# One-hot rows of the PEER gate matrix move from GpSimd to VectorE and ScalarE; row gathers run five ahead

## The chip, the cores and the metric

The kernel runs on one core of one Trainium2 chip. The metric is device time in microseconds (us), the median of several executions. A core has five engines with an instruction queue each: TensorE (PE in the profile; PEld is its weight load), VectorE (DVE), ScalarE (ACT), GpSimd (POOL), and the DMA queue's own engine SyncE (SP). Each engine works through its queue strictly in order and waits on semaphores for what other engines or transfers must deliver.

## The reference

Two transformer blocks over 512 tokens of width 1024 (the second one two layers deep). The change touches one part of the first block, a PEER feed-forward with 16384 experts of one row each. Cut to that part:

```python
q  = (hn @ w_query).reshape(b, s, 8, 2, 128)
sc = einsum('bshcd,hckd->bshck', q, sub_keys)        # 8 heads, 2 x 128 keys
v1, i1 = top_k(sc[..., 0, :], 16);  v2, i2 = top_k(sc[..., 1, :], 16)
cand = v1[..., :, None] + v2[..., None, :]           # 256 pairs, 16 best kept
top, pos = top_k(cand.reshape(..., 256), 16)
idx  = i1 * 128 + i2 at pos;  gate = softmax(top)    # 8 x 16 experts per token
act  = gelu(einsum('bld,blhkd->blhk', hn, expert_down[idx]))
out  = einsum('blhk,blhkd->bld', gate * act, expert_up[idx])
```

So every token picks 128 of 16384 experts, takes a dot product with each one's down row, and sums their up rows with weight gate times gelu.

## The kernel before

The first 128 tokens (`GAT`) are done by **gathering**: for each of the 128 slots one indirect DMA fetches 128 down rows (512 KB, one per token), VectorE multiplies and reduces them against `hn` (line 1049), and after 128 such steps 128 more fetch the up rows, which VectorE adds into `racc` (line 1058). GpSimd issues these gathers (line 1045), with a ring of four `rows` buffers, so a gather may only be issued when the row four steps earlier has been consumed.

The other 384 tokens (`DENSE`) are done **densely**: all 16384 experts are computed. `peer_down` runs 128 dense rows; a dense row streams 512 KB of down weights through SyncE's queue, splits them into a high part on ScalarE (`whi`, line 267) and a low part on VectorE (`wlo`, line 268), runs 24 matmuls of 128x384 (lines 272 to 274), applies Gelu on ScalarE (line 1124) and writes 192 KB of `actd` to DRAM from ScalarE's DMA queue (line 1125). Then `peer_up` runs 16 groups of 8 tiles, each tile again 24 matmuls, with the `actd` values multiplied by a gate matrix read back from DRAM (`gd`, line 1162).

That **gate matrix** is 128 x 128 per token, and `peer_gates` builds it during the dense rows of `peer_down`: per token a one-hot matrix `oa` (line 1280) and a one-hot matrix scaled by the gates, `ob` (line 1282), each 128x128, are multiplied on TensorE (line 1283, two matmul instructions per token in the trace). Four tokens form a quad; a quad fills one PSUM bank that ScalarE copies out (`gst`, line 1284). 96 quads are needed, 384 tokens. After each 32 tokens GpSimd issues a 2 MB write to `gd` (line 1286). Of the four `oa` of a quad GpSimd makes three and VectorE one; all four `ob` are VectorE's.

The order on the queues: `hidden()` yields four pieces per dense row; after each piece the gate and routing work gets `PACE` credits (a quad costs 2.2, a routing step its yielded cost), and the gather generator `rows` gets 0.27 of a step. A tile scheduler then places the instructions on each engine by its own estimate of when they are ready, and may move gathers forward. In `peer_up` each tile is followed by 1.25 gather steps.

At the hand-over, the `at` and `gt` loads of the first `peer_up` group go through GpSimd's queue, behind the gathers that stand before them there, and TensorE's first `peer_up` matmul needs them.

Of the kernel before, what the change touches and what calls it, by code (L numbers as in the profile page):

```python
# [10 lines left out]
F32 = mybir.dt.float32  # L11
# [3 lines left out]
AF = mybir.ActivationFunctionType  # L15
ALU = mybir.AluOpType
# [6 lines left out]
D = 1024  # L23
# [12 lines left out]
FAR = CAP * (NEXP + 2)  # L36
FULL = (6, 11)
RAW = 20
PACE = 0.62
GAT = 128  # L40
DENSE = S - GAT

# [177 lines left out]
class Kernel:  # L220
# [813 lines left out]
    def gathered(self, st):  # L1034


        V, A, P, p = self.V, self.A, self.P, st["pool"]
        act = p.tile([128, 128], F32, name="ract")
        steps = [(name, k) for name in ("rows_down", "rows_up") for k in range(128)]
        ahead = []  # L1040
        for i, (name, k) in enumerate(steps):
            while len(ahead) < 4 and i + len(ahead) < len(steps):
                n, kk = steps[i + len(ahead)]
                r = p.tile([128, D], F32, name="rows", bufs=4)
                P.indirect_dma_start(r, None, self.I[n], bass.IndirectOffsetOnAxis(ap=st["idx"][:, kk:kk + 1], axis=0))  # L1045
                ahead.append(r)
            r = ahead.pop(0)
            if name == "rows_down":
                V.tensor_tensor_reduce(out=r, in0=r, in1=st["hn"], scale=1.0, scalar=0.0, op0=ALU.mult, op1=ALU.add,
                                       accum_out=act[:, k:k + 1])  # L1050
            else:
                if k == 0:
                    A.activation(act, act, AF.Gelu)
                    V.tensor_mul(act, act, st["gate"])
                    acc = p.tile([128, D], F32, name="racc", tag="rhn")
                    V.tensor_scalar(acc, r, act[:, 0:1], None, op0=ALU.mult)
                else:
                    V.scalar_tensor_tensor(acc, r, act[:, k:k + 1], acc, op0=ALU.mult, op1=ALU.add)  # L1058
            yield
        for h in range(2):  # L1060
            tr = self.ps("t", [128, 4, 128])
            for k in range(4):
                self.transpose(tr[:, k], acc[:, (4 * h + k) * 128:(4 * h + k + 1) * 128])
            x = self.x[:, 4 * h:4 * h + 4, :GAT]
            V.tensor_add(x, x, tr)

    def peer_down(self, actd, gd, TG, st, rows):

        V, A, P, T, Q, I = self.V, self.A, self.P, self.T, self.Q, self.I
        with self.pool("u2") as up:  # L1070
# [12 lines left out]
            with self.pool("pk", 1) as p1:  # L1083
# [23 lines left out]
                with self.pool("pk2", 2) as p2:  # L1107
# [18 lines left out]
                    for i, _ in enumerate(hidden()):  # L1126
                        credit += PACE
                        while credit > 0:
                            credit -= next(work, 1.0e9)
                        if st["ready"]:  # L1130
                            due += 0.27
                            while due >= 1:
                                next(rows, None)
                                due -= 1
                    _run(work)

    def peer_up(self, actd, gd, TG, rows):
        V, A, P, T, Q, I = self.V, self.A, self.P, self.T, self.Q, self.I
        with self.pool("pu", 2) as p2:
# [28 lines left out]
            for g in range(16):  # L1168
                hi, lo = _run(nxt)
                nxt = weighted(g + 1) if g < 15 else iter(())  # L1170
                for j in range(KC):
# [4 lines left out]
                        self.mm3(ps, (whi[:, sl], wlo[:, sl]), (hi[:, k], lo[:, k]), k == 0, k == 7)  # L1176
                    next(nxt, None)
                    V.tensor_add(self.x[:, j, GAT:], self.x[:, j, GAT:], ps)
                    due += 1.25
                    while due >= 1:  # L1180
                        next(rows, None)
                        due -= 1
# [86 lines left out]
    def peer_gates(self, c, sT, p2, gd, TG):  # L1269
# [3 lines left out]
        for j in range(128 // TG):  # L1273
            st = p2.tile([128, 128, TG], F32, name="gst")
            for t4 in range(TG // 4):
                ps = self.ps("ts"[t4 % 2], [128, 4, 128])
                for i in range(4):
                    t = j * TG + t4 * 4 + i
                    oa = p2.tile([128, 128], F32, name="oa", bufs=10)
                    (V if i == 3 else P).tensor_scalar(oa, iota, sT[:, 1, t:t + 1], None, op0=ALU.is_equal)  # L1280
                    ob = p2.tile([128, 128], F32, name="ob", bufs=10)
                    V.tensor_scalar(ob, iota, sT[:, 0, t:t + 1], sT[:, 2, t:t + 1], op0=ALU.is_equal, op1=ALU.mult)
                    T.matmul(ps[:, i], lhsT=oa, rhs=ob, start=True, stop=True)
                A.activation(st[:, :, t4 * 4:t4 * 4 + 4], ps.rearrange("p t i -> p i t"), AF.Copy)
# [827 lines left out]
```

## Time and profile before

| | us |
|---|---|
| median of 3 executions (lowest to highest) | 4601.32 (4599.44 to 4601.47) |
| the profiled execution's own time | 4597.02 |
| its span, first to last instruction | 4595.2 |
| TensorE busy in the span | 4302.3 (94%) |
| VectorE busy | 2733.3 (59%) |
| ScalarE busy | 1342.6 (29%) |
| GpSimd busy | 1489.9 (32%) |

The busy shares are means over stages of different kinds. The dense rows of `peer_down` run from about 945 us to 1673 us of the span, the gate matrix is built from 1088 us to 1556 us, and `peer_up` runs from 1704 us to about 2245 us. A window of the trace gives the busy time of each engine in one stretch, the granted TensorE clock (1.00 is 2.4 GHz, 0.50 is 1.2 GHz), and how busy the DMA engines were. Matmuls overlap, so the mean duration of one is longer than its share of the busy time.

### The profile page before, as it was taken

To read this page: it belongs to the slowest core of one execution; us is meant where nothing else is said; L and a number is where in the kernel's file an instruction comes from. 1 tells how busy PE (TensorE), PEld (TensorE's weight loads), DVE (VectorE), ACT (ScalarE), POOL (GpSimd) and SP (SyncE) were. 2 spreads that over 40 slices of the span, in tenths; PEclk is the share of its full clock that TensorE was granted. 3 is DMA by queue.
4 is the path that set the end of the run, shared out by engine and by line. 5 is a ranking of instruction groups with operands and counts; after the bars stand their busy time and mean duration, and the time that the engine had idled before them with its cause. 6 is when DMAs were issued, how large, how long until landed. Compare 5 with 4: busy or idle time off the path is not lost. (4 is left out here: it accounts for less than half of the span.)

```text
span 4595.2 us, 59880 instructions
## 1 busy us (share of the span) xinstructions
PE 4302.3 (94%) x21607; PEld 3280.4 (71%) x21607; DVE 2733.3 (59%) x5252; ACT 1342.6 (29%) x2195; POOL 1489.9 (32%) x1171
## 2 busy tenths in 40 slices
PE   8998989998899879999999998999989999899997
PEld 7787778897889869999877675444448778545443
DVE  6577775798877679997457775221234665522122
ACT  5324442343333323333333332000123433200001
POOL 2153345019999654342113451000011346100000
PEclk9999999999999989999999998999999999899998
DMA  4133433347778899996333446989862122598985
GB/s 155 50 103 109 128 113 112 108 141 253 274 275 300 316 350 350 340 334 237 118 116 114 138 133 223 364 321 346 319 256 85 61 67 95 218 353 325 350 311 236
DMA packets 351615, 987.39 MB, mean 215 GB/s; under 512 B 34288, under 2 KB 114672, under 8 KB 349392
## 3 DMA queue, kind: packets, MB, share of 16 engines
q1 hardware_dynamic: 293488, 795.77, 48.6%
q0 software_dynamic: 39392, 162.55, 9.9%
q10 hardware_dynamic: 18432, 25.17, 1.5%
q8 instruction: 174, 2.85, 0.3%
q14 instruction: 129, 1.06, 0.1%
HBM read 926.70 MB, written 56.66 MB: 214 GB/s over the span
## 5 line engine op out<-in xcount | busy, mean ns | idle before, releaser
L267 ACT ACTIVATE whi<-raw 128x1024 fp32r<-128x1024 f32 (+3 forms) x582 | 569.0, 979 | 1307.0 <-PE acc L273 780.2
L268 DVE TENSOR_TENSOR wlo<-raw,whi 128x1024 fp32r<-128x1024 f32 (+4 forms) x438 | 535.6, 1225 | 231.7 <-ACT whi L267 224.9
L1746 PE MATMUL acc<-raw,xg 128*64 128x512 f32 (+1 forms) x2024 | 554.7, 599 | 0.0
L349 POOL TENSOR_TENSOR ssq<-ssq,sq 128x512 f32<-128x512 f32 (+1 forms) x22 | 31.5, 1442 | 1337.1 <-ACT sq L348 1336.8
L272 PE MATMUL acc<-hn_hi,whi 128*128 128x384 f32 (+1 forms) x1152 | 406.5, 354 | 9.0 <-ACT act L1124 9.0
L274 PE MATMUL acc<-hn_hi,wlo 128*128 128x384 f32 (+1 forms) x1152 | 402.1, 350 | 13.5 <-DVE wlo L268 13.5
L268 POOL TENSOR_TENSOR wlo<-raw,whi 128x1024 fp32r<-128x1024 f32 (+3 forms) x144 | 281.1, 1954 | 373.9 <-ACT whi L267 363.7
L273 PE MATMUL acc<-hn_lo,whi 128*128 128x384 f32 (+1 forms) x1152 | 402.1, 349 | 0.0
L272 PE MATMUL acc<-c_hi,whi 128*128 128x384 f32 x1024 | 342.7, 336 | 30.2 <-ACT c_hi L267 30.2
L1746 PEld LDWEIGHTS acc<-raw,xg 128*64 128x64 f32 (+1 forms) x2024 | 164.0, 140 | 284.2 <-issue 260.8
L273 PE MATMUL acc<-c_lo,whi 128*128 128x384 f32 x1024 | 343.4, 335 | 0.6 <-DVE c_lo L268 0.6
L274 PE MATMUL acc<-c_hi,wlo 128*128 128x384 f32 x1024 | 342.4, 335 | 0.8 <-DVE wlo L268 0.8
L1280 POOL TENSOR_SCALAR oa<-const,sT 128x128 f32<-128x128 f32 x288 | 269.1, 946 | 2.8
L1794 DVE SCALAR_TENSOR_TENSOR x<-t,mod,x 128x512 f32<-128x512 f32 x160 | 117.4, 749 | 250.0 <-PE t L1792 250.0
L463 DVE RECIPROCAL gate<-gate 128x512 f32<-128x512 f32 x72 | 241.0, 3347 | 36.7 <-POOL gate L462 36.6
L1045 POOL DMA_INDIRECT rows<-in_rows_up_dram,ridx x128 | 172.1, 1345 | 257.3 <-DVE racc L1058 241.4
L1768 PE MATMUL acc<-raw,h 128*64 128x512 f32 (+1 forms) x1000 | 251.5, 597 | 3.9 <-ACT h L1757 3.9
L274 PEld LDWEIGHTS acc<-hn_hi,wlo 128*128 128x128 f32 x1152 | 221.9, 193 | 21.5 <-DVE wlo L268 16.7
L272 PEld LDWEIGHTS acc<-hn_hi,whi 128*128 128x128 f32 x1152 | 222.9, 194 | 15.4 <-ACT act L1124 10.1
L273 PEld LDWEIGHTS acc<-hn_lo,whi 128*128 128x128 f32 x1152 | 222.7, 193 | 5.0 <-issue 0.2
L272 PEld LDWEIGHTS acc<-c_hi,whi 128*128 128x128 f32 x1024 | 193.1, 189 | 30.5 <-ACT c_hi L267 30.5
L272 PE MATMUL acc<-h_hi,whi 128*128 128x512 f32 x512 | 213.3, 417 | 0.4 <-ACT whi L267 0.4
(672 smaller groups left out, 9620.0 us busy)
## 6 DMA issues: line engine op xcount, KB each, us to landing
raw<-in_w_dram SPq DMA_DIRECT2D x756, 512.0 KB
raw<-in_down_dram SPq DMA_DIRECT2D x128, 512.0 KB
raw<-in_up_dram SPq DMA_DIRECT2D x128, 512.0 KB
raw<-in_ada_dram SPq DMA_DIRECT2D x96, 512.0 KB
raw<-in_w_gate_dram SPq DMA_DIRECT2D x72, 512.0 KB
actd<-act ACTq DMA_DIRECT2D x128, 192.0 KB
gd<-gst POOLq DMA_DIRECT2D x12, 2048.0 KB
gt<-gd SPq DMA_DIRECT2D x30, 768.0 KB
```

What stands on the lines that cost most here:

```text
L267: self.A.activation(hi, src, AF.Copy)
L268: (self.P if engine == "ap" else self.V).tensor_sub(lo, src, hi.bitcast(F32))
L272: T.matmul(out, lhsT=l[0], rhs=r[0], start=start, stop=False)
L273: T.matmul(out, lhsT=l[0], rhs=r[1], start=False, stop=False)
L274: self.last = T.matmul(out, lhsT=l[1], rhs=r[0], start=False, stop=stop)
L349: (eng or (self.V if k % 2 else self.P)).tensor_add(self.ssq[k % 2], self.ssq[k % 2], sq)
L463: V.reciprocal(d, d)
L1045: P.indirect_dma_start(r, None, self.I[n], bass.IndirectOffsetOnAxis(ap=st["idx"][:, kk:kk + 1], axis=0))
L1280: (V if i == 3 else P).tensor_scalar(oa, iota, sT[:, 1, t:t + 1], None, op0=ALU.is_equal)
L1746: T.matmul(ps[i * m:(i + 1) * m], lhsT=xg[:, kk, o + i * m:o + (i + 1) * m], rhs=w[i][:, k * 512:(k + 1) * 512], start=kk == 0, stop=kk == 7)
L1768: T.matmul(po[h][i * m:(i + 1) * m], lhsT=hh[:, f, i * m:(i + 1) * m], rhs=w[i][:, h * 512:(h + 1) * 512], start=f == 0, stop=f == 3)
L1794: V.scalar_tensor_tensor(self.x[:, k], ps, mod[:, 40 + k:41 + k], self.x[:, k], op0=ALU.mult, op1=ALU.add)
```

## The change

The one-hot `oa` leaves GpSimd. Of the four tokens of a quad, two `oa` are made by VectorE with the same comparison as before, and two by ScalarE in two instructions: `od = |index - position|`, then `oa = relu(1 - od)`, which is 1 where the index matches and 0 elsewhere. The `oa` and `ob` rings shrink from ten buffers to eight, and `od` has two. The gathers get a fifth `rows` buffer and run five ahead. `PACE` rises from 0.62 to 0.68. Once the gate work is finished, the gather generator gets 0.5 of a step per piece in place of 0.27, and in `peer_up` 1.1 in place of 1.25 per tile.

```diff
-PACE = 0.62
+PACE = 0.68
@@ gathered
-            while len(ahead) < 4 and i + len(ahead) < len(steps):
+            while len(ahead) < 5 and i + len(ahead) < len(steps):
-                r = p.tile([128, D], F32, name="rows", bufs=4)
+                r = p.tile([128, D], F32, name="rows", bufs=5)
@@ peer_down
-                            due += 0.27
+                            due += 0.27 if credit > -1e8 else 0.5
@@ peer_up
-                    due += 1.25
+                    due += 1.1
@@ peer_gates
-                    oa = p2.tile([128, 128], F32, name="oa", bufs=10)
-                    (V if i == 3 else P).tensor_scalar(oa, iota, sT[:, 1, t:t + 1], None, op0=ALU.is_equal)
-                    ob = p2.tile([128, 128], F32, name="ob", bufs=10)
+                    oa = p2.tile([128, 128], F32, name="oa", bufs=8)
+                    if i % 2:
+                        V.tensor_scalar(oa, iota, sT[:, 1, t:t + 1], None, op0=ALU.is_equal)
+                    else:
+                        od = p2.tile([128, 128], F32, name="od", bufs=2)
+                        A.activation(od, iota, AF.Abs, scale=-1.0, bias=sT[:, 1, t:t + 1])
+                        A.activation(oa, od, AF.Relu, scale=-1.0, bias=self.onec)
+                    ob = p2.tile([128, 128], F32, name="ob", bufs=8)
```

On GpSimd's queue, in the middle of the stage that builds the gate matrix, one-hot comparisons (`oa`) stand between the gathers (`rows`) before:

```order
L1045 DMA rows<-in_rows_down_dram,ridx 128x1024
L1280 TENSOR_SCALAR oa<-const,sT 128x128 x3
L1045 DMA rows<-in_rows_down_dram,ridx 128x1024
L1280 TENSOR_SCALAR oa<-const,sT 128x128 x2
L1045 DMA rows<-in_rows_down_dram,ridx 128x1024
L1280 TENSOR_SCALAR oa<-const,sT 128x128 x4
```

In the changed kernel the same stretch of GpSimd's queue reads as follows, with the products of the routing (`oh`) and the 2 MB writes (`gd`):

```order
L1045 DMA rows<-in_rows_down_dram,ridx 128x1024 x4
L1292 DMA gd<-gst 128x4096
L1045 DMA rows<-in_rows_down_dram,ridx 128x1024 x5
L1253 TENSOR_TENSOR oh<-oh,idxf 128x256 x4
L1045 DMA rows<-in_rows_down_dram,ridx 128x1024 x6
L1253 TENSOR_TENSOR oh<-oh,idxf 128x256 x4
```

The comparisons are gone from the queue, and the gathers follow each other.

On ScalarE's queue, in the same stage, a stretch of before, with the split of the weights (`whi`), the Gelu (`act`) with its write, and the copies of finished quads (`gst`):

```order
L1284 ACTIVATE gst<-t 128x128x4
L1284 ACTIVATE gst<-s 128x128x4
L267 ACTIVATE whi<-raw 128x1024
L1124 ACTIVATE act_6210<-acc 128x384
L1125 DMA actd<-act_6210 128x384
```

In the changed kernel:

```order
L267 ACTIVATE whi<-raw 128x1024
L1286 ACTIVATE oa<-od,onec 128x128 x2
L1290 ACTIVATE gst<-t 128x128x4
L1285 ACTIVATE od<-const,sT 128x128 x2
L1290 ACTIVATE gst<-s 128x128x4
L1286 ACTIVATE oa<-od,onec 128x128
L1124 ACTIVATE act_6209<-acc 128x384
```

The 384 small instructions stand between the instructions of the dense rows, behind waits of these. No table load is added.

On VectorE's queue, after the last gate instruction and before the hand-over to `peer_up`, gathered up rows (into `racc`) stand between the low parts of the dense rows (`wlo`); before:

```order
L268 TENSOR_TENSOR wlo_14136<-raw_14133,whi_14135 128x1024
L1058 SCALAR_TENSOR_TENSOR racc_14453<-rows_14817,ract_7654,racc_14453 128x1024
L268 TENSOR_TENSOR wlo_14172<-raw_14169,whi_14171 128x1024
L1058 SCALAR_TENSOR_TENSOR racc_14453<-rows_14855,ract_7654,racc_14453 128x1024
L1058 SCALAR_TENSOR_TENSOR racc_14453<-rows_14858,ract_7654,racc_14453 128x1024
L268 TENSOR_TENSOR wlo_14208<-raw_14205,whi_14207 128x1024
```

In the changed kernel:

```order
L268 TENSOR_TENSOR wlo_14117<-raw_14114,whi_14116 128x1024
L1058 SCALAR_TENSOR_TENSOR racc_14371<-rows_14580,ract_7627,racc_14371 128x1024
L1058 SCALAR_TENSOR_TENSOR racc_14371<-rows_14604,ract_7627,racc_14371 128x1024
L268 TENSOR_TENSOR wlo_14156<-raw_14153,whi_14155 128x1024
L1058 SCALAR_TENSOR_TENSOR racc_14371<-rows_14619,ract_7627,racc_14371 128x1024
L1058 SCALAR_TENSOR_TENSOR racc_14371<-rows_14643,ract_7627,racc_14371 128x1024
```

One or two gathered rows per dense row have become two.

## Rows read from the trace of the kernel before

**Rows 1.** Busy time of each engine by stretch, granted clock, DMA share, GB/s.

```profile
core 0: us, PE busy (x) PEld busy (x) DVE busy (x) ACT busy (x) POOL busy (x), PEclk, DMA share, GB/s
...
1088.00:1556.00 468.00, 414.81 (x2473) 401.31 (x2473) 377.97 (x795) 155.62 (x235) 435.72 (x430) 0.96 0.78 278
1556.00:1590.00 34.00, 26.38 (x153) 25.74 (x153) 19.60 (x27) 10.82 (x17) 15.49 (x13) 0.98 0.94 355
1590.00:1670.00 80.00, 78.65 (x438) 78.17 (x439) 56.25 (x48) 25.98 (x36) 41.46 (x30) 0.97 0.97 351
1670.00:1710.00 40.00, 9.23 (x37) 8.40 (x36) 26.30 (x25) 6.58 (x14) 24.96 (x21) 0.59 0.95 334
1710.00:2200.00 490.00, 489.22 (x2822) 488.87 (x2820) 429.53 (x506) 177.15 (x238) 183.07 (x142) 1.00 0.89 309
1750.00:1950.00 200.00, 200.00 (x1155) 200.00 (x1155) 186.40 (x217) 73.44 (x100) 82.34 (x67) 1.00 0.97 341
```

**Rows 2.** Waits in 1088:1556: who waited for whom, us in total, times, longest.

```profile
DVE rows L1049 <- DMA rows<-in_rows_down_dram,ridx: 60.5, 34, 6.7
...
PE s L1283 <- POOL oa L1280: 26.3, 21, 3.2
PE t L1283 <- POOL oa L1280: 20.1, 19, 3.7
...
DVE ob L1282 <- PE t L1283: 9.0, 6, 3.3
DVE wlo L268 <- ACT whi L267: 8.8, 6, 3.7
...
DVE ob L1282 <- PE s L1283: 3.0, 5, 1.2
```

**Rows 3.** Groups in 1088:1556: count, busy us, mean ns, idle before and its releaser.

```profile
L1280 POOL TENSOR_SCALAR oa<-const,sT 128x128 f32<-128x128 f32 x286 | 267.7, 948 | 2.7
L272 PE MATMUL acc<-hn_hi,whi 128*128 128x384 f32 x568 | 201.2, 354 | 0.0
...
L1049 DVE CUSTOM_DVE_ANT_0 rows<-rows,rhn 128x1024 f32<-128x1024 f32 x105 | 136.3, 1301 | 60.7 <-DMA rows<-in_rows_down_dram,ridx 60.5
L1282 DVE TENSOR_SCALAR ob<-const,sT 128x128 f32<-128x128 f32 x384 | 132.0, 393 | 12.3 <-PE t L1283 9.0 <-PE s L1283 3.0
...
L268 DVE TENSOR_TENSOR wlo<-raw,whi 128x1024 fp32r<-128x1024 f32 x74 | 91.1, 1231 | 8.8 <-ACT whi L267 8.8
...
L1280 DVE TENSOR_SCALAR oa<-const,sT 128x128 f32<-128x128 f32 x96 | 34.4, 358 | 3.1 <-PE s L1283 3.0
```

**Rows 4.** Single lines: shortest, median and longest duration in ns, first and last start.

```profile
L1280 DVE TENSOR_SCALAR oa<-const,sT x96: 267/315/777, 1089.1 to 1548.9; 128x128 f32<-128x128 f32 x96
L1282 DVE TENSOR_SCALAR ob<-const,sT x384: 328/340/831, 1088.2 to 1549.3; 128x128 f32<-128x128 f32 x192
L1049 DVE CUSTOM_DVE_ANT_0 rows<-rows,rhn x128: 1206/1220/4392, 1044.1 to 1587.7; 128x1024 f32<-128x1024 f32 x128
L1045 POOL DMA_INDIRECT rows<-in_rows_down_dram,ridx x128: 937/1052/3350, 1037.8 to 1579.9; - x128
L1045 POOL DMA_INDIRECT rows<-in_rows_up_dram,ridx x128: 932/1011/4022, 1582.7 to 2087.9; - x128
```

**Rows 5.** ScalarE, 128x128 from SBUF with a per-partition bias, elsewhere in the program.

```profile
L790 ACT ACTIVATE dw<-dw,mx 128x128 f32<-128x128 f32 x36 | 14.0, 390 | 15.0 <-DVE mx L788 15.0
...
L1511 ACT ACTIVATE e<-e,nm 128x128 f32<-128x128 f32 x8 | 3.2, 397 | 1.9 <-DVE nm L1510 1.6 <-DVE ls L1517 0.2
```

**Rows 6.** What the DMA engines moved in 1088:1556 (first) and 1556:1710 (second).

```profile
DMA packets 36982, 130.03 MB, mean 278 GB/s; under 512 B 4100, under 2 KB 12804, under 8 KB 35539
...
DMA packets 16958, 53.50 MB, mean 347 GB/s; under 512 B 1840, under 2 KB 5748, under 8 KB 16822
```

**Rows 7.** The hand-over, 1590:1720: TensorE's longest wait and GpSimd's.

```profile
POOL rows L1045 <- DVE racc L1058: 47.9, 27, 3.5
...
PE acc L272 <- ACT c_hi L267: 30.2, 1, 30.2
```

**Rows 8.** Gathered up rows on VectorE in 1710:1950 of `peer_up` (busy, count).

```profile
1710.00:1950.00 240.00, 65.52 (x50) 1.00 0.98 345
```

## The prediction

> **What bounds the kernel now.** I read the table by stretch first, then the waits of the stretch that the change touches, then the groups and the transfers there. The profiled execution took 4597.0 us; the median of the runs is 4601.3, 4.3 us above it, so the sum is made against 4597.0 and 4.3 is added at the end.
>
> The change works in one part. While the gate matrix is built (1088 to 1556 us), TensorE is busy 414.8 of 468 us and GpSimd 435.7, or 93% [rows 1]. TensorE idles 53 us there. 46.4 us of it are two rows: its matmuls `s` and `t` wait for GpSimd's `oa` (26.3 + 20.1) [rows 2]. GpSimd spends 267.7 us on 286 `oa`, 948 ns each [rows 3]. So GpSimd is the bound of this stretch; VectorE (378.0 us) idles 90, 60.5 of it for gathered rows [rows 1, 2], which GpSimd issues between the `oa`.
>
> Behind it the bound is another. From 1590 to 1670 us TensorE is busy 78.7 of 80 us, but the DMA engines are at 0.97 of their time with 351 GB/s; from 1670 to 1710 us TensorE has 9.2 of 40 us of work at DMA share 0.95, and waits 30.2 us for the first operand of `peer_up`, made of `at`, whose load stands on GpSimd's queue behind gathers that wait for `racc` [rows 1, 7]. In `peer_up` TensorE is busy 489.2 of 490 us [rows 1]: nothing that other engines save there shortens the run.
>
> **Part 1, the gate stretch: 468 becomes 416 us.** The order of before puts 71 dense rows (568 matmuls of each kind over 8, [rows 3]) and 103 gathered rows between the first and the last gate instruction, the order of the changed kernel 64.5 and 114; the 96 quads stay. `PACE` does that.
> TensorE: at full clock 1155 matmuls take 200 us [rows 1], 0.173 us each, 24 to a dense row, so 4.16 us. 6.5 rows less are 27 us, and 414.8 becomes 388. This is the floor of the stretch.
> VectorE: 378.0, plus 96 `oa` at 0.358 us (34.4), plus 11 gathered rows at 1.30 us and their 0.08 us accumulator reads (15), less 6 `wlo` at 1.231 (7) [rows 1, 3], is 420 us. That is the upper bound. These are durations beside a busy GpSimd: `ob` has a mean of 393 and a median of 340 ns, the gathered row 1301 and 1220, `oa` 358 and 315 [rows 3, 4]. All at their medians would take off 384 x 0.053 + 114 x 0.081 + 192 x 0.043 = 38 us, and 382 is the lower bound. GpSimd loses 267.7 of its 435.7 us, 61%, so I take 0.61 x 38 = 23 off: 397 us.
> So VectorE comes to lie just above TensorE and leads. Its idle time: the 60.5 us for gathered rows I drop, because a gather no longer queues behind `oa`, the ring is one deeper, and from 1556 on, without many `oa`, a gather follows its row; the bound is 0 to 60.5. The waits for a free `ob` buffer (9.0 + 3.0) [rows 2] stay, the ring being shorter. 8.8 us for `whi` [rows 2] overlap with what TensorE still has in front of it; I keep 7. 397 + 12 + 7 = 416, bounds 388 and 502 (420 with all waits of rows 2). Gain 52 us.
> ScalarE: the trace has no Abs or Relu; the nearest rows, 128x128 from SBUF with a bias per partition, take 390 to 397 ns [rows 5]. 384 x 0.397 = 152 us on 155.6 busy [rows 1] is 308 of 416 us, 74%. It costs nothing in the sum as long as `oa` is early: on ScalarE's queue nearly all `oa` come after a `whi` that can run at least one dense row (some 6 us) before TensorE uses them. If that cover is gone, the wait of TensorE for `oa` stays with a new owner (a rival below).
> GpSimd keeps gathers, routing products and `gd` writes, some 168 us, and is no bound.
>
> A row against the change: VectorE now runs twice the comparisons beside GpSimd's gather issues. In the trace a gather issue has a median of 1052 ns beside them and 1011 ns in the later stage that has none [rows 4], so they delay it little. The Trainium skill, "SBUF — State Buffer", section "Who interferes with whom", says that a `tensor_scalar` in VectorE's two-port mode and a GpSimd instruction exclude each other from a shared port pair for the whole instruction, and its section "SBUF: two separate sides" warns that VectorE can so keep GpSimd from writing the descriptors of its DMAs. By the rule VectorE's excess of 38 us over the medians goes almost wholly with GpSimd's `oa`, which would make Part 1 about 15 us shorter than my sum; the longest gather issues of 3350 ns fit the warning, the medians do not.
>
> **Part 2, the dense rows behind it: 40 us are given back.** 31 dense rows now follow the last quad instead of 25, and the gathers beside them rise from 41 over 27 `wlo` (1.52 per row) to 64 over 32 (2.0). A dense row moves 0.524 MB of weights and 0.197 MB of `actd`, a gather 0.524 MB: 1.77 MB per dense row instead of 1.52. The DMA engines moved 351 GB/s at a share of 0.97 [rows 1], so 362 at 1.0: 4.89 us per dense row, above TensorE's 4.16. VectorE meets the gathered rows in its queue ahead of the next `wlo`, so TensorE follows. 31 x 4.89 = 152 us against 117 (1556 to 1673): +35. At the hand-over 14 gathered rows instead of 11 stand between the last `wlo` and the first `at` product; 3 x 1.28 is +4, and the last `gd` write adds 1. Together +40. The check by bytes: 6 dense rows and 26 gathered rows more are 18 MB on 53.5 MB that took 154 us [rows 6], +50 at 351 GB/s; the lower bound is TensorE's 31 x 4.16 = 129 us, +12 (+16 with the hand-over).
>
> **Part 3, `peer_up`: 0.** 50 gathered rows over 47 tiles remain, instead of 86 over 94. VectorE is busy 186.4 of 200 us [rows 1] with 50 rows in 240 us [rows 8], 0.87 per tile; 1.06 per tile adds 0.25 us to 3.88 of 4.16. It just fits, and TensorE's operands are three buffers ahead. I take 0, up to 8 us lost. Afterwards VectorE and DMA have less to do, which gains nothing. The routing before 1088 us has the same work, and its first quad comes at dense row 32.5 instead of 32: 0.
>
> **Sum.** 4597.0 - 52 + 40 = 4585.0; plus 4.3, rounded: 4589 us, 0.27% below 4601.3. A difference of 0.2% (9.2 us) is about what a measurement of this kernel tells from no change.
>
> **The rivals.**
> *The tail costs little.* Weights and gathers are separate queues; if the DMA engines carried the 425 GB/s that 1.77 MB in 4.16 us ask for, TensorE would set the pace: +16 instead of +40, Part 1 between 416 and 400 (TensorE's floor and 12): 4601.3 - 52 + 16 = 4565, or 4549. For it: TensorE was full at 1.5 gathers per row [rows 1]. Against: a share of 0.97 leaves no room for 2.0.
> *VectorE takes GpSimd's place* (slower). Its 420 us are not relieved, and half of the 60.5 us wait for gathers stays, because 114 gathers and the 2 MB `gd` writes share GpSimd's DMA queue at 330 GB/s: 420 + 30 + 12 + 9 = 471, so +3 + 40: 4644. It decides from a stretch of 428 us, 31 us of idle time on 397 of VectorE or 8 on 420. For it: VectorE idles 90 us today. Against: the gathers' reason to be late was GpSimd's queue.
> *The wait changes owner.* ScalarE's queue serves `whi` and Gelu, both waiting for TensorE, ahead of `oa`; if all 46.4 us of `oa` wait stay, the stretch is 388 + 53 = 441, -27 + 40: 4614. For it: 384 more instructions in an ordered queue, 74% busy. Against: the lead of a row.
> That the change does not do what it says is excluded: the order has no `oa` on GpSimd and no added table load.
>
> **How the numbers follow.** Forecast 0.46 (4575 to 4602; 0.28 of it faster, 0.18 within 0.2%); cheap tail 0.22, faster; VectorE 0.19, slower; owner 0.13 (0.08 within, 0.05 slower). Faster 0.50, same 0.26, slower 0.24. The range goes to the lower end of the cheap tail, 4549, and up to 4624, where VectorE's rival is half way to its price: outside remain some 0.07 below and 0.11 above. The forecast's own range is 4575 to 4602.
>
> **What would show it.** Right: in the gate stretch the waits of TensorE for `oa` fall from 46 to under 15 us, VectorE is busy over 90%, its wait for gathered rows is under 20 us, `ob` comes near 340 ns, and the stretch from the first to the last quad is 405 to 428 us; then some 31 dense rows take near 4.9 us each at a DMA share of 0.95 or more, and the gap before `peer_up` is 30 to 42 us; `peer_up` takes 540 us as before. Wrong: a gate stretch above 428 us (which wait leads then, for `oa` from ScalarE, for gathers, or for `ob`, names the rival), dense rows at 4.2 us behind it, or idle time of TensorE in the first third of `peer_up`.

## The result, and the profile of the changed kernel

The changed kernel takes 4564.35 us (median of 4 runs, 4563.66 to 4570.65) against 4600.38 us of the kernel before in the same comparison: a ratio of 0.9927 with a 95% interval of 0.9910 to 0.9944, or 36 us less. The forecast was 12 us less. The profiled execution took 4570.65 us with a span of 4568.8 us; it is the slowest of the four, 6.3 us above their median.

Busy time of each engine by stage (the columns are those of [rows 1]): the gate stretch, the dense rows behind it, the hand-over, and `peer_up`:

```profile
core 0: us, PE busy (x) PEld busy (x) DVE busy (x) ACT busy (x) POOL busy (x), PEclk, DMA share, GB/s
1088.00:1473.00 385.00, 368.88 (x2339) 362.43 (x2339) 380.18 (x906) 261.83 (x607) 180.37 (x154) 0.99 0.93 342
1473.00:1629.40 156.40, 133.49 (x743) 127.77 (x742) 115.81 (x94) 45.06 (x62) 91.03 (x64) 1.00 0.98 363
1629.40:1660.00 30.60, 0.03 (x1) 0.00 (x0) 20.16 (x18) 2.87 (x6) 20.51 (x19) 0.56 0.98 345
1660.00:2205.50 545.50, 538.77 (x3083) 535.51 (x3083) 408.15 (x496) 195.73 (x263) 147.31 (x112) 0.99 0.75 255
```

The gate stretch takes 385 us instead of 468 [rows 1]. TensorE idles 16 us in it, not 53, and GpSimd is busy 180 of 385 us, not 436 of 468. VectorE is busy 380.2 of 385 us, 99%. Behind it things get worse: TensorE idles 23 of 156 us, where the shorter stage of before had 9; what it waits for there is shown under e3.

What TensorE and VectorE wait for in the gate stretch of the changed kernel (who waited for whom, us in total, times, longest):

```profile
PE acc L274 <- DVE wlo L268: 10.5, 10, 4.3
...
PE acc L272 <- ACT act L1124: 3.6, 3, 1.6
...
DVE oa L1281 <- PE s L1289: 2.3, 5, 0.8
...
PE s L1289 <- DVE ob L1288: 1.6, 2, 1.0
```

The waits of `s` and `t` for `oa` on GpSimd, 46.4 us in [rows 2], have no successor: none on ScalarE's `oa` is among them. What is left of TensorE's waiting is for VectorE's `wlo`.

The costliest groups of VectorE and the two new ones of ScalarE in that stretch (count, busy us, mean ns of one, idle before):

```profile
L1049 DVE CUSTOM_DVE_ANT_0 rows<-rows,rhn 128x1024 f32<-128x1024 f32 x114 | 139.3, 1233 | 0.6 <-DMA rows<-in_rows_down_dram,ridx 0.6
L1288 DVE TENSOR_SCALAR ob<-const,sT 128x128 f32<-128x128 f32 x384 | 128.2, 371 | 0.0
...
L268 DVE TENSOR_TENSOR wlo<-raw,whi 128x1024 fp32r<-128x1024 f32 x67 | 81.7, 1222 | 0.0
L1286 ACT ACTIVATE oa<-od,onec 128x128 f32<-128x128 f32 x190 | 72.8, 394 | 37.4 <-PE t L1289 32.3 <-PE s L1289 3.8 <-ACT act L1124 0.4
L1285 ACT ACTIVATE od<-const,sT 128x128 f32<-128x128 f32 x188 | 70.4, 395 | 4.3 <-DVE sT L1266 2.6
...
L1281 DVE TENSOR_SCALAR oa<-const,sT 128x128 f32<-128x128 f32 x192 | 58.3, 306 | 3.7 <-PE s L1289 2.3 <-PE t L1289 1.4
```

Set beside [rows 3], VectorE's idle time before a gathered row has gone from 60.7 to 0.6 us. Records of neighbouring VectorE instructions overlap, so busy time over count is the net price of one: `oa` went from 358 to 304 ns (34.4 over 96, 58.3 over 192), `ob` from 344 to 334, a gathered row from 1298 to 1222.

**Where the 26 us of the two profiled spans are.** From 1088 us, about where the first gate product stands, to the end of `peer_up` the kernel before needs 1154.5 us and the changed one 1117.5: gate stretch -83, rows behind it +39, hand-over 0, `peer_up` +7. Everything behind `peer_up`, where the code is the same, took 10.6 us more in this one execution. Over all the profiled kernels below that compute the same, that last part took between 2353 and 2367 us, so 10.6 us is scatter, and it is why the two spans differ by less than the medians.

The 37 us can be cut another way. TensorE executes the same matmuls in both (6166 and 6165 records), but is busy for 1060.8 us before and 1041.2 after. So 17 us are idle time and 20 us are matmuls that run faster. The granted clock fits that: 0.96 against 0.99 in the gate stretch, 0.97 against 1.00 in the rows behind it. One place in the kernel before shows how it is lost (TensorE from 1541 us: start, duration, instruction, idle before it):

```profile
1541.84 1.22 PE L1283 MATMUL t<-ob,oa 128*128 128x128 f32 x4 [3.71 <-POOL oa L1280]
1542.85 0.63 PE L1283 MATMUL s<-ob,oa 128*128 128x128 f32 x2
1544.23 0.80 PE L1283 MATMUL s<-ob,oa 128*128 128x128 f32 x2 [0.75 <-POOL oa L1280]
1544.68 0.67 PE L272 MATMUL acc<-hn_hi,whi 128*128 128x384 f32 x1
1545.15 0.52 PE L273 MATMUL acc<-hn_lo,whi 128*128 128x384 f32 x1
...
1547.39 0.47 PE L274 MATMUL acc<-hn_hi,wlo 128*128 128x384 f32 x1
1547.70 0.33 PE L272 MATMUL acc<-hn_hi,whi 128*128 128x384 f32 x1
```

After 3.71 us of waiting the dense matmuls start 0.32 us apart and last 0.52 us: the granted clock from 1541.8 to 1547.4 us is 0.50, the lower of its two levels (1.2 GHz). From 1547.7 us they last 0.33 us and start 0.17 us apart, at a granted clock of 1.00 (2.4 GHz). This wait cost its own length and the slow matmuls behind it. Not every wait does: the waits of 1.35 us behind the gate stretch of the changed kernel (e3) leave the granted clock at 1.00.

### The profile page after: what moved, and what is told of

Its sections match the earlier page's. It is cut to its first block, busy times and chain, and to the rows that moved or that the text cites. A ratio compares the mean times of both kernels' runs of the same rounds, so it can differ in the third digit from the quotient of the medians.

```text
span 4568.8 us, 59963 instructions
## 1 busy us (share of the span) xinstructions
PE 4298.5 (94%) x21607; PEld 3271.1 (72%) x21607; DVE 2732.7 (60%) x5348; ACT 1457.4 (32%) x2579; POOL 1227.5 (27%) x883
## 5 line engine op out<-in xcount | busy, mean ns | idle before, releaser
L268 POOL TENSOR_TENSOR wlo<-raw,whi 128x1024 fp32r<-128x1024 f32 (+3 forms) x144 | 281.7, 1958 | 376.2 <-ACT whi L267 369.4
L272 PE MATMUL acc<-c_hi,whi 128*128 128x384 f32 x1024 | 342.7, 336 | 30.9 <-ACT c_hi L267 30.7
L1045 POOL DMA_INDIRECT rows<-in_rows_down_dram,ridx x128 | 168.6, 1317 | 188.2 <-DVE ract L1049 95.8
```

Source lines behind the costliest of these rows:

```text
L268: (self.P if engine == "ap" else self.V).tensor_sub(lo, src, hi.bitcast(F32))
L272: T.matmul(out, lhsT=l[0], rhs=r[0], start=start, stop=False)
```

## The experiments

All of them change either the kernel before or the changed kernel. The table gives what the four stages lasted, with TensorE's idle time in brackets, and the ratio to the kernel before in the same comparison with its 95% interval. The gate stretch runs from the first to the last gate product; its idle time is counted from 1088 us. The stage times come from one profiled execution of each kernel.

| kernel | gate stretch | rows behind | hand-over | peer_up | ratio |
|---|---|---|---|---|---|
| before | 468.2 (53) | 116.5 (9.0) | 30.2 | 538.9 (1.4) | 1 |
| changed | 381.8 (16) | 157.3 (22.9) | 30.7 | 545.4 (6.6) | 0.9927 (0.9910 to 0.9944) |
| e1 one-hots only | 398.9 (10) | 113.3 (5.3) | 30.3 | 536.9 (0.6) | 0.9835 (0.9808 to 0.9862) |
| e2 pacing and ring only | 444.2 (67) | 177.5 (23.0) | 30.8 | 553.6 (11.5) | 1.0103 (1.0074 to 1.0132) |
| e3 changed, ring of 4 | 375.0 (8) | 133.5 (5.5) | 28.9 | 539.9 (2.5) | 0.9830 (0.9806 to 0.9853) |
| e4 changed, idle comparisons | 445.8 (53) | 148.8 (18.7) | 34.4 | 550.8 (7.9) | 1.0045 (1.0031 to 1.0059) |
| e5 e3, loads on ScalarE's queue | 376.2 (9) | 133.0 (5.4) | 28.1 | 541.3 (3.2) | 0.9832 (0.9815 to 0.9850) |
| e6 e3, three `oa` on ScalarE | 367.6 (10) | 142.1 (3.4) | 29.8 | 536.7 (0.6) | 0.9828 (0.9808 to 0.9848) |
| e7 before, no gathers | 420.5 (6) | 95.7 (0) | 3.9 | 535.6 (0.9) | not compared |
| e8 changed, ring of 3 | 364.5 (5) | 134.2 (0) | 20.0 | 539.5 (1.6) | 0.9798 (0.9778 to 0.9817) |
| e9 e8, loads on ScalarE's queue | 363.6 (6) | 134.2 (0) | 17.6 | 542.3 (4.3) | 0.9782 (0.9768 to 0.9797) |
| e10 e9, three `oa` on ScalarE | 371.4 (9) | 134.1 (0) | 18.9 | 539.6 (2.0) | 0.9781 (0.9768 to 0.9795) |
| e11 before, ring of 3 | 462.7 (42) | 100.6 (3.1) | 19.4 | 538.2 (1.9) | 0.9935 (0.9914 to 0.9957) |

How many dense rows fall into the first and how many into the second column differs between kernels, since the scheduler places them; only their sum is fixed. The idle times can be compared.

### e1: only the one-hot rows move

```diff
 (changed kernel)
-PACE = 0.68
+PACE = 0.62
-            while len(ahead) < 5 and i + len(ahead) < len(steps):
+            while len(ahead) < 4 and i + len(ahead) < len(steps):
-                r = p.tile([128, D], F32, name="rows", bufs=5)
+                r = p.tile([128, D], F32, name="rows", bufs=4)
-                            due += 0.27 if credit > -1e8 else 0.5
+                            due += 0.27
-                    due += 1.1
+                    due += 1.25
-                    oa = p2.tile([128, 128], F32, name="oa", bufs=8)
+                    oa = p2.tile([128, 128], F32, name="oa", bufs=10)
-                    ob = p2.tile([128, 128], F32, name="ob", bufs=8)
+                    ob = p2.tile([128, 128], F32, name="ob", bufs=10)
```

> Only the one-hot rows move (half to VectorE, half to ScalarE); pacing, ring of four gathers and ten oa/ob buffers are as before. On VectorE's queue 72 dense rows lie between the first and the last gate instruction and 27 with 46 gathered rows behind it, so the stage behind the gate work is that of the kernel before. Theory A (the moved one-hot rows bring the whole gain, and the fifth gather buffer takes part of it back, because more gathers stand beside the last dense rows): the gate stretch falls from 468 to about 400 us (369 us of TensorE in the changed kernel plus six dense rows at 4.16), the rows behind it take 117 us, peer_up 538 us as before; about 4530 us, some 35 below the changed kernel. Theory B (pacing and ring bring a share of the gain): above 4564 us.

4525.66 us, ratio 0.9835: theory A by its time; by what way the fifth buffer costs its part is seen under e3. The one-hot rows alone bring twice what the whole change brings. TensorE's idle time falls by 43 us in the gate stretch and by 4 behind it, and `peer_up` is undisturbed.

### e2: only the pacing and the ring

```diff
 (kernel before)
-PACE = 0.62
+PACE = 0.68
-            while len(ahead) < 4 and i + len(ahead) < len(steps):
+            while len(ahead) < 5 and i + len(ahead) < len(steps):
-                r = p.tile([128, D], F32, name="rows", bufs=4)
+                r = p.tile([128, D], F32, name="rows", bufs=5)
-                            due += 0.27
+                            due += 0.27 if credit > -1e8 else 0.5
-                    due += 1.25
+                    due += 1.1
```

> GpSimd keeps its one-hot rows; PACE 0.68, the ring of five gathers, 0.5 and 1.1 are those of the changed kernel. In the order 61 dense rows lie in the gate stretch, and 37 rows with 77 gathered rows behind it. Theory A (GpSimd's comparisons bound the stretch, gathers price the rows behind it): gate stretch about 455 us, 37 rows at 4.9 us are 181 us instead of 117, peer_up loses 7; about 4655 us. Theory B (the pacing is a gain by itself): below 4590 us.

4648.38 us, 1.0% slower than before: theory A by its time, within 7 us. Its parts miss by more and partly cancel: the gate stretch is 11 us shorter than expected, and `peer_up` loses 15 us instead of 7. TensorE idles 67 us in the gate stretch, 23 behind it, 11.5 in `peer_up`. So this half of the change is a loss by itself.

### e3: the changed kernel with a ring of four

```diff
-            while len(ahead) < 5 and i + len(ahead) < len(steps):
+            while len(ahead) < 4 and i + len(ahead) < len(steps):
-                r = p.tile([128, D], F32, name="rows", bufs=5)
+                r = p.tile([128, D], F32, name="rows", bufs=4)
```

> The changed kernel with four gather buffers instead of five, nothing else. In the order 32 dense rows still follow the gate work, but with 49 gathered rows up to the last of them instead of 64, and 81 rather than 50 gathered rows fall into peer_up. Theory A (the rows behind the gate work are slow because of the bytes of the gathers beside them): 32 rows at the 4.33 us per row of the kernel before (117 over 27) are 139 us instead of 156, peer_up takes 538 instead of 545 us; about 4540 us. Theory B (the rows are slow for another reason, such as Gelu's place in ScalarE's queue): 4560 to 4568 us.

4525.24 us: 15 us below theory A's 4540. The stage behind the gate work fell to 133.5 us (139 expected) and `peer_up` to 539.9 (538 expected); not foreseen was that the gate stretch gets 7 us shorter as well, with some ten gathered rows fewer in it (114 and 105 on VectorE). The stretch and the stage behind it, to be set beside the first two lines of the changed kernel:

```profile
1088.00:1459.20 371.20, 362.78 (x2338) 359.62 (x2337) 364.72 (x870) 259.19 (x598) 159.85 (x143) 1.00 0.91 338
1459.20:1592.00 132.80, 127.29 (x727) 125.37 (x725) 92.13 (x89) 43.81 (x60) 59.74 (x49) 1.00 0.97 360
```

The DMA engines work at a share of 0.97 and 360 GB/s here, 0.98 and 363 in the changed kernel: nearly full both times. Yet TensorE does not wait for transfers in this stage. Its only waits there, in the changed kernel (with VectorE's for gathered rows) and in e3:

```profile
PE acc L272 <- ACT act L1124: 22.9, 17, 1.3
...
DVE racc L1058 <- DMA rows<-in_rows_up_dram,ridx: 0.2, 1, 0.2
```

```profile
PE acc L272 <- ACT act L1124: 5.4, 4, 1.3
```

All 22.9 us stand in front of the first matmul of a dense row and wait for a Gelu on ScalarE, which empties an accumulator; the code has four (`acc`). One of the 17 on TensorE, then the same moment on ScalarE's queue, in the changed kernel (start, duration, instruction, idle before):

```profile
1623.30 0.34 PE L274 MATMUL acc<-hn_hi,wlo 128*128 128x384 f32 x1
1624.98 0.44 PE L272 MATMUL acc<-hn_hi,whi 128*128 128x384 f32 x1 [1.35 <-ACT act L1124]
```

```profile
1623.50 1.06 ACT L267 ACTIVATE whi<-raw 128x1024 fp32r<-128x1024 f32 x1 [3.10 <-PE acc L273]
1624.46 0.47 ACT L1124 ACTIVATE act<-acc 128x384 f32<-128x384 f32 x1
```

The Gelu stands behind a split (`whi`) that waits for TensorE to finish a row: all 31 splits of the stage start 0.04 to 0.05 us after the end of a row's last matmul of line 273, so none of them waits for weights. Split and Gelu then run, and TensorE starts 0.05 us after the Gelu. Each of the 17 waits is 1.35 us long. At 1549 us, before one of them, TensorE still has 16 rows to run and ScalarE 20 Gelus: all four accumulators are full.

So the fifth buffer cost TensorE its time through the order in which the scheduler put ScalarE's queue: with five buffers the Gelus behind the gate work mostly stand in pairs behind two splits, with four mostly one behind each split. The run alone can't tell theory A from theory B, since the ring changes the transfers and that order together; the waits show the cause that theory B names, Gelu's place, though the time is not the one it gave. e2, the other kernel with five buffers, has the same row in this stage, 22.9 us in 17 waits, and e8, with three, has none. Why the scheduler orders so stays open, and no run shows what the transfers would have cost with the Gelus in another order.

The ring also answers which constant made the gathers denser. In the order (none of these kernels was run) of a kernel with 0.27, 0.12 or 0 in place of 0.5, the same 32 dense rows and 78 gathered rows follow the gate work, and with 0 and 0.7 in place of 1.1 too: the scheduler moves a gather up as soon as a buffer is free, whatever the rate says. With four buffers there are 60, with three 49. So 0.5 and 1.1 do nothing to this stage, and the depth of the ring does it all.

### e4: comparisons on GpSimd that nobody reads

```diff
 (changed kernel, per quad)
+                for i in range(2):
+                    ox = p2.tile([128, 128], F32, name="ox", bufs=2)
+                    P.tensor_scalar(ox, iota, sT[:, 1, t:t + 1], None, op0=ALU.is_equal)
```

> The changed kernel with two more comparisons per quad on GpSimd, 192 in all, whose results nobody reads. GpSimd is then busy 180 + 192 x 0.948 = 362 us in the stretch, not its bound, and TensorE doesn't wait for them. Theory A (a GpSimd comparison takes time from VectorE beside it): VectorE's ob, oa and gathered rows get longer again, by two thirds of the difference between the two traces: 26 us x 0.67 = 17 us on 380, and VectorE leads, so about 4580 us, with a net gathered row of 1270 ns instead of 1222. Theory B (GpSimd's comparisons cost only the waiting for them): durations as in the changed kernel, 4560 to 4568 us. In either, gathered rows that come late because GpSimd's queue is longer would show as VectorE waiting for them, which is read apart.

4623.98 us: both theories miss. The stretch is 64 us longer than in the changed kernel. Waits in it (who waited for whom, us in total, times, longest), then VectorE's groups:

```profile
DVE rows L1049 <- DMA rows<-in_rows_down_dram,ridx: 48.1, 24, 5.2
...
PE acc L274 <- DVE wlo L268: 23.7, 7, 7.3
...
PE t L1289 <- DVE ob L1288: 10.1, 7, 4.2
...
PE s L1289 <- DVE ob L1288: 9.2, 5, 4.7
```

```profile
L1288 DVE TENSOR_SCALAR ob<-const,sT 128x128 f32<-128x128 f32 x384 | 132.8, 384 | 1.8 <-PE s L1289 1.3 <-PE t L1289 0.5
...
L1281 DVE TENSOR_SCALAR oa<-const,sT 128x128 f32<-128x128 f32 x192 | 63.0, 334 | 0.0
```

VectorE waits 48.1 us for gathered rows, 0.6 in the changed kernel, and what stands behind them on its queue (`wlo`, `ob`) reaches TensorE late. The slowing of VectorE itself is real but small: `ob` is at 346 ns net (132.8 over 384) instead of 334, `oa` at 328 instead of 304, 9 us in all. One place on GpSimd's queue shows how such a wait comes about (start, duration, instruction, idle before):

```profile
1315.39 2.17 POOL L1045 DMA_INDIRECT rows<-in_rows_down_dram,ridx  x1 [0.17 <-DVE oa L1281]
1317.59 8.45 POOL L1292 TENSOR_SCALAR ox<-const,sT 128x128 f32<-128x128 f32 x9
1326.21 1.03 POOL L1045 DMA_INDIRECT rows<-in_rows_down_dram,ridx  x1 [0.17 <-DVE oa L1281]
```

Nine comparisons, 8.45 us, stand in front of one gather, and VectorE idles 4.29 us for a gathered row up to 1330.64 us. GpSimd is busy 354 of 448 us in the stretch, 79%, and not a bound by its sum; the order on its queue makes gathers late. That all of the 48 us come about so was not traced wait by wait.

### e7: the kernel before without gathers

```diff
 (kernel before, gathered)
+        return
+        yield
```

> The kernel before without the gathers of the first 128 tokens (their rows are not fetched, not multiplied and not added): GpSimd keeps its three one-hot rows per quad. Theory A (the comparisons hurt because they stand between the gathers, so that VectorE waits for gathered rows and everything behind it comes late): TensorE's waits for GpSimd's oa fall from 46 to under 10 us and the stretch goes to the busy time of TensorE, 72 rows, about 395 us. Theory B (GpSimd's one-hot rows come late by themselves, 948 ns each in an ordered queue): the waits for oa stay above 25 us, the stretch above 415 us. The total isn't to be compared, because the up rows are left out too.

Nearer to theory A, but not at its numbers. TensorE's waits for GpSimd's `oa` over the whole stretch (all lines stand two further down in this kernel), then the stretch and the hand-over:

```profile
PE t L1285 <- POOL oa L1282: 8.2, 8, 1.8
PE s L1285 <- POOL oa L1282: 3.1, 6, 0.8
```

```profile
1068.00:1490.00 422.00, 411.02 (x2611) 405.71 (x2612) 258.83 (x581) 165.49 (x250) 245.81 (x327) 1.00 0.53 188
...
1584.80:1588.70 3.90, 0.04 (x2) 0.03 (x1) 2.22 (x5) 1.91 (x4) 0.00 (x0) 1.00 0.47 152
```

The waits are 11.3 us, just above theory A's 10 and far below theory B's 25. The stretch is 420.5 us long, more than either theory has for it, but not by waiting: it holds some 77 dense rows (2611 matmuls less the 768 of the gate products, 24 to a row) and not 72, and TensorE is busy 411.0 of 422 us at full clock. So comparisons without gathers hold up little, and by e4 comparisons that nobody reads hold up TensorE once gathers stand behind them. The run left out VectorE's gathered rows, the gathers' traffic (DMA share 0.53) and GpSimd's own time for issuing them too (GpSimd is busy 246 of 422 us, 58%, against 93% before), so it doesn't say how much of the relief is each one's. In the kernel before both hold, a queue that is nearly full and an order that mixes the two kinds of work, and no run parts them. The last line is a by-product: without gathers the hand-over lasts 3.9 us instead of 30.2.

### e8 and e11: a ring of three

```diff
-            while len(ahead) < 5 and i + len(ahead) < len(steps):
+            while len(ahead) < 3 and i + len(ahead) < len(steps):
-                r = p.tile([128, D], F32, name="rows", bufs=5)
+                r = p.tile([128, D], F32, name="rows", bufs=3)
```

> The changed kernel with three gather buffers instead of five. In the order 65 dense rows and 89 gathered rows lie in the gate stretch, 34 rows with 44 gathered rows behind it (1.3 per row), 5 gathered rows at the hand-over instead of 14, and 106 rows over 115 tiles in peer_up. Theory A (fewer gathers beside the last dense rows are the gain): 34 rows at 4.17 us, and an idle time of about 21 us at the hand-over, 8 less than with four; about 4515 us. Theory B (three buffers are too few for rows that land 8 us after their issue): VectorE waits over 20 us for gathered rows in the gate stretch; 4535 us or more.

4505.4 us, ratio 0.9798: nearer to theory A by its time (about 4515), and with that 59 us below the changed kernel. The three stages up to `peer_up`:

```profile
1088.00:1448.00 360.00, 354.97 (x2284) 350.70 (x2283) 344.89 (x837) 257.20 (x594) 147.97 (x130) 1.00 0.90 326
1448.00:1581.50 133.50, 133.47 (x770) 133.15 (x769) 88.22 (x100) 47.02 (x65) 51.74 (x42) 1.00 0.95 347
1581.50:1601.50 20.00, 0.03 (x1) 0.04 (x1) 9.32 (x10) 1.96 (x3) 13.14 (x12) 0.59 0.92 323
```

The stage behind the gate work has no idle time at all any more, no Gelu keeps TensorE waiting there, and the hand-over is 20.0 us (21 expected). The wait of theory B is there, but smaller than it needs: 14.4 us of VectorE for gathered rows in the gate stretch.

The same ring in the kernel before (e11: 3 instead of 4 in the same two lines):

> The kernel before with three gather buffers instead of four; GpSimd keeps its one-hot rows. In the order 74 dense rows and 99 gathered rows lie in the gate stretch, 25 rows with 31 gathered rows behind it, 6 rows at the hand-over instead of 11. Theory A (the depth of the ring acts on the rows behind the gate work and on the hand-over alone): 25 rows at 4.17 us instead of 27 at 4.31, idle time 21 instead of 30 us, the stretch longer by its two rows; about 4585 us. Theory B (gathers that are issued late by a busy GpSimd need the ring as a reserve): VectorE waits clearly more than the 60.5 us of the kernel before for gathered rows in the stretch, and the total is above 4600 us.

4572.95 us, ratio 0.9935: better than either theory. VectorE's wait for gathered rows rises from 60.5 to 79.9 us as theory B says, yet the stretch is 5 us shorter with two dense rows more, and the hand-over falls to 19.4 us. TensorE's wait for `oa` fell from 46.4 to 35.0 us; why VectorE's longer wait doesn't reach it stays open. One number in the kernel before would have brought nearly what the change brings.

### e5, e6, e9, e10: what more there is to take

e5 puts the first `at` and `gt` loads of `peer_up` on another queue, e9 does the same with a ring of three:

```diff
-                    queue = P if g == 0 else Q
+                    queue = A if g == 0 else Q
```

> The changed kernel with four gather buffers, and the first at and gt loads of peer_up on ScalarE's queue instead of GpSimd's. In the run with four buffers the last actd write was issued at 1600.1 us, the at load at 1609.4 us behind gathers, and TensorE stood idle for 28.9 us. Theory A (the place on GpSimd's queue costs the time): the load is issued some 9 us earlier, the idle time falls to 20 to 22 us, since VectorE still has gathered rows in front of the first product; about 4517 us. Theory B (the load lands late wherever it is issued, the DMA engines being full): 4523 to 4527 us.

> Three gather buffers, and the first at and gt loads on ScalarE's queue. With four buffers that load was issued early and TensorE's idle time stayed at 28 us, because VectorE had eleven gathered rows and their transfers in front of the first product. With three buffers five rows stand there, and they were done at 1595.5 us while the product started at 1600.3, behind loads issued at 1591.0. Theory A (of the two, gathered rows and loads, the later one decides): here the load is the later one, so an issue at 1583.6 gives back the 4 to 5 us up to VectorE's rows: idle time 15 to 16 us instead of 20.0, about 4501 us. Theory B (the gathers use up the transfers' time wherever the load is issued): 20 us idle, 4505 us.

In e5 the loads were issued at 1606.9 us, right behind the last `actd` write, and still the hand-over lasted 28.1 us (4525.78 us: theory B). VectorE's queue tells why (start, duration, instruction, idle before):

```profile
1616.57 1.28 DVE L1058 SCALAR_TENSOR_TENSOR racc<-rows,ract,racc 128x1024 f32<-128x1024 f32 x1 [0.67 <-DMA rows<-in_rows_up_dram,ridx]
1621.58 1.28 DVE L1058 SCALAR_TENSOR_TENSOR racc<-rows,ract,racc 128x1024 f32<-128x1024 f32 x1 [3.73 <-DMA rows<-in_rows_up_dram,ridx]
1623.45 1.28 DVE L1058 SCALAR_TENSOR_TENSOR racc<-rows,ract,racc 128x1024 f32<-128x1024 f32 x1 [0.59 <-DMA rows<-in_rows_up_dram,ridx]
1624.65 1.02 DVE L1162 TENSOR_TENSOR at<-at,gt 128x384 f32<-128x384 f32 x2
```

The first product stands behind gathered rows, and these now wait for transfers that share the DMA engines with the loads. The hand-over follows the number of gathers in it: 3.9 us with none, 20.0 with five rows behind the last `wlo` (e8), 19.4 with six (e11), 28.1 to 30.3 with eleven (before, e1, e3, e5, e6), 30.7 to 34.4 with fourteen (changed, e2, e4). In e9 the loads, with fewer gathers beside them, gained 2.4 us in the one profiled execution (17.6 instead of 20.0) and not the 4 to 5 of theory A; the time (4505.85 us) is that of theory B and is not told apart from e8.

e6 and e10 give ScalarE three of four one-hot rows:

```diff
-                    if i % 2:
+                    if i == 3:
                         V.tensor_scalar(oa, iota, sT[:, 1, t:t + 1], None, op0=ALU.is_equal)
```

> The changed kernel with four gather buffers, and three of four one-hot rows oa on ScalarE, one on VectorE. VectorE loses 96 x 0.31 = 30 us, ScalarE gains 75 on 259. The order has 64 dense rows in the gate stretch and 35 behind it. Theory A (with VectorE relieved TensorE alone leads, ScalarE has room): 8 us of idle time of TensorE in the stretch go at most, the rest only shifts rows; 4517 to 4522 us. Theory B (ScalarE, then some 93% busy and waiting for TensorE in its queue, hands oa over late): TensorE waits for oa from ScalarE, above 4535 us.

> The same as the run before it, and three of four one-hot rows on ScalarE. Theory A (TensorE leads the gate stretch: with three buffers it is busy 355.0 of 360.0 us there): at most 5 us less than with two of four, 4496 to 4501 us. Theory B (ScalarE's longer queue makes one-hot rows late): above 4505 us.

4522.26 and 4504.08 us, neither told apart from its partner (e3, e9). The first is at the upper end of theory A's 4517 to 4522, the second lies between the two theories (up to 4501, above 4505). In e6 VectorE falls from 365 of 371 to 345 of 369 us and TensorE idles 10 us instead of 8; ScalarE at 306 of 369 us is no bound. VectorE at 99% in the changed kernel was therefore near the end of what it could cost: with gathered rows or comparisons taken off it (e3, e6, e8, e9, e10), TensorE's idle time goes from 16 us to between 5 and 10 and no further.

## Why the prediction was right in direction and too small

**Part 1, the gate stretch (416 us predicted, 385 measured): the mis-sized term.** Three numbers in it were too high. TensorE's floor, 414.8 less 27, was taken at 388 us and measured 369: the 414.8 of [rows 1] were busy time at a granted clock of 0.96, and the prediction carried slow matmuls over into the floor, although it priced a matmul at full clock one sentence earlier. When the waits went, the clock came back to 0.99, near the 1.00 of `peer_up`. VectorE was taken at 397 and measured 380, at its lower bound of 382: the excess over the medians went whole and not by 61%. The idle time was taken at 19 us and measured 5. VectorE does lead, as predicted, but just above a floor that lies 19 us lower.

**GpSimd as the bound.** The prediction read GpSimd's 93% and TensorE's 46.4 us of waiting for `oa` as GpSimd being the bound of the stretch. The waiting did vanish, and dropping the 60.5 us for gathered rows was right (0.6 measured). e4 shows that a full queue is not needed for it: at 79% of GpSimd's time the order of comparisons and gather issues on one queue costs TensorE as much, 53 us, by another way, over gathered rows that come late to VectorE. How much of the 53 us in the kernel before is GpSimd's full time and how much its order stays open (e7).

**The port rule.** The net price of VectorE's `ob`, `oa` and gathered rows fell by 3 to 15% when GpSimd's comparisons went, and e4 brings a part of it back (346 and 328 ns). In e7, with comparisons on GpSimd and no gathers, `ob` and `oa` cost 342 and 361 ns (130.8 us over 383, 34.7 over 96), as in the kernel before, so it is the comparisons that go with the dearer price. The Trainium skill, "SBUF — State Buffer", section "Who interferes with whom", states that VectorE in a two-port mode and GpSimd exclude each other for a whole instruction. By that rule the prediction's Part 1 would have been about 15 us shorter, and the trace agrees in size: VectorE is busy 380 instead of 397 us. That it comes about by this exclusion no run here shows. The other side, late descriptors for GpSimd's DMAs, doesn't show: with twice the comparisons on VectorE its wait for gathered rows was 0.6 us, and a gather issue of down rows had a median of 1016 ns, against 1052 before.

**Part 2, the rows behind it (+40 predicted, +39 measured): the size met, the cause not.** The prediction let the DMA engines set the pace, at 4.89 us per dense row, passed on to TensorE by gathered rows ahead of `wlo` on VectorE's queue. Measured were 156.4 us for 743 matmuls, 31 rows at 5.05 us, at a DMA share of 0.98. But VectorE waited 0.2 us for gathered rows, and TensorE's only waits, 22.9 us, were for Gelus behind splits on ScalarE's queue (e3). Of the 39 us more, 25 are TensorE's own work (133.5 us busy instead of 108.0, for 743 matmuls instead of 607) and 14 its idle time (22.9 instead of 9.0). That 39 stands beside 40 is luck: of the 40, 35 were for the rows and 5 for the hand-over, which stayed where it was (30.7 instead of 30.2 us). The prediction also put the denser gathers down to the change's rates; it is the fifth buffer.

**Part 3, `peer_up` (0, up to 8 lost): 7 lost**, in its first third, where the DMA share is 1.01; within the bound that was given, though idle time of TensorE in this place was also named as a sign of being wrong. The idle time there goes with the ring too (6.6, 2.5 and 1.6 us with five, four and three).

**The sum.** 52 less 40 should have been 83 less 39 and 7: 37 us, next to the 36 of the medians. The rival of a cheap tail came to nearly the measured time (4565 us) by the wrong way: the tail was as dear as forecast. The measured 4564 us lie below the forecast's own 4575 to 4602 and inside the whole range only because that was drawn down for this rival. The gate stretch, 382 us from first to last product, also missed the 405 to 428 that were to show the forecast right, on the side of a larger gain. VectorE's rival needed idle time that didn't come, and ScalarE's `oa` never held up TensorE.

## What to carry to other kernels

An in-order queue that issues latency-bound gathers should not also do arithmetic that others don't need there: a comparison of under 1 us, placed nine at a time in front of a gather, stalled a third engine. A busy time read at a reduced clock is no floor; work it out from matmuls at the full clock, and look behind a long wait for slow matmuls that go with it. The depth of a prefetch ring is a rate control when the scheduler issues whatever has a buffer, and it can reach queues that have nothing to do with the prefetch: here three and four buffers beat five (ratios 0.980, 0.983 and 0.993), and the largest part that was traced was TensorE's wait for Gelus behind splits on ScalarE's queue, 22.9 us with five buffers, 5.4 with four, none with three. A stage whose transfers run at a share of 0.98 is not for that reason bound by them; ask what the waiting engine waits for.

## What the runs showed of the hardware that was not expected

About half of the gain from the first gate product to the end of `peer_up` is clock: 6166 matmuls took 1060.8 us of TensorE before and 6165 took 1041.2 after, with a granted clock of 0.96 and 0.99 in the gate stretch. On ScalarE the one-hot in two instructions cost 394 and 395 ns for 128x128, as the biased instructions of [rows 5] had it, whichever function they ran. On GpSimd a comparison of 128x128 took 772 ns in the mean without gathers on its queue and 948 with them.
